# A hybrid transformer layer on one core: GpSimd's block sums, the banks of the down products, a chunk's final weighing and a weight split put elsewhere

## The chip, the cores and the metric

The kernel runs on one core of one Trainium2 chip. Its time is the device time of one execution in microseconds (us). A core has a matrix engine (TensorE, PE in the rows; PEld is its weight load), a vector engine (VectorE, DVE), a scalar engine (ScalarE, ACT), GpSimd (POOL) and SyncE (SP), which here issues all DMAs. Each engine takes its own instructions in order and waits on semaphores of the others. Matrix products land in PSUM, eight banks of 512 float32 columns on 128 partitions. GpSimd has no way to PSUM in this kernel.

## The reference

One encoder layer over 1024 prompt tokens and 64 sample tokens, all in float32. What follows the attention is what matters here:

```python
x = x + (1.0 + ada[2]) * (o @ w_o)
h = rmsnorm(x, g_ffn) * (1.0 + ada[4]) + ada[3]
f = (jax.nn.silu(h @ w_gate) * (h @ w_up)) @ w_down     # 1024 -> 2816 -> 1024
x = x + (1.0 + ada[5]) * f
y = rmsnorm(x, g_final)
```

## The kernel before

**Tokens and products.** x lies transposed, as eight tiles of 128 features (m or kt = 0 to 7), in three chunks c of 384, 384 and 320 tokens. Each float32 matrix product is made of three: every operand is split into a rounded high part and the rest (`whi`, `wlo` for a weight, `h`, `d` and so on for an activation), and PE adds high x high, low x high and high x low into one bank. A split of a weight is a cast on ScalarE (`whi`), then a subtraction on VectorE or GpSimd (`wlo`). A weight tile of 128 x 1024 or 128 x 512 elements comes by one or two DMAs into one of four `wraw` buffers, and the split parts rotate through three pairs of tiles.

**Output projection.** `out_block(g, mp, chunks, ...)` takes one 512 x 256 block of w_o, splits it (on GpSimd for the four blocks of the second half, `OPL`), and makes its products for the chunks named, 24 matmuls a chunk. At the end of it chunk 2's rows are normed for the FFN (`norm2_last`), while the blocks of chunk 1 and then those of chunk 0 are made, so that three blocks of w_o are loaded and split twice.

**First FFN pass, chunk 2.** Eleven groups g of two 128-wide FFN columns: gate and up products (24 matmuls each), `silu`, the product `d`, its split, then `down_begin` and eight `down_block`s, one for each m, of six matmuls. `down_begin` makes the first half of three blocks ahead, in the banks t, t, acc. VectorE adds the finished block into x (line 1202). In group 0 the rows of chunks 0 and 1 get their root-mean-square: `token_cols` sums over features on PE (bank u), VectorE and ScalarE make the reciprocal root, `spread` lays it over 128 partitions with PE. In the last group `weigh` squares and scales each finished x for the final norm, on ScalarE, with the sum of squares on GpSimd.

**Second FFN pass, chunks 0 and 1.** Eleven groups again. The two chunks and the two columns make 2 x 2 blocks, multiplied in seven products of 12 matmuls instead of eight (`Seven`, `Blocks`). The weights' side needs block sums, all on GpSimd: `sums_first` (lines 1320 and 1321), `sum2` (1324) and `sum4` (1327); `prep` then splits an operand (line 1166 on ScalarE, 1167 on VectorE). After the seven gate products come seven up products, i = 0 to 6, whose `evac` (lines 1362 to 1374) and `up` (1506: product with silu; 1508: cast; 1509: low part) make `d`. A low part is queued in `left` and issued at the next `later(left)`. Then 16 down blocks follow, chunk 1 first, bi = 0 to 15. The two splits of w_down stand in the up products: at i == 3 on VectorE, at i == 5 with its low part on GpSimd. `final_cols`, `final_last` and `final_tile` norm, transpose and write the output.

**Order.** Up to the FFN a scheduler of the framework sets each engine's order. From `in_order` on it is the order in which the code is written, for PE, ScalarE, VectorE and GpSimd, up to `in_order.__exit__`; what follows that is the scheduler's again. Banks are asked for by tag: z (three), t (two), acc, u, av (one each).

## Time and profile before

| | |
|---|---|
| time, median of 3 runs (lowest to highest) | 1706.82 us (1706.05 to 1712.06) |
| the profiled execution: its own time | 1706.56 us |
| its span on the core | 1704.8 us |
| busy: PE, PEld | 1561.3 us (92%), 1449.6 us (85%) |
| busy: DVE, ACT, POOL | 1129.8 us (66%), 808.6 us (47%), 850.6 us (50%) |
| TensorE clock granted, mean | 0.97 of full speed |
| matmuls | 9558 |

Times in the rows are microseconds from the start of the span. The attention ends at about 817 us, the output projection's second half and `norm2_last` run to about 876, the first FFN pass to about 1133, the second to about 1693, and the last output is written after that. Busy time of PE is modelled from pipelined matmuls, so a wait of PE is better read from the list of waits (who waited, for whom, how long in total, how many times, the longest) than from the busy share.

### The profile page before, as it was taken

To read this page: it belongs to the slowest core of one execution; us is meant where nothing else is said; L and a number is where in the kernel's file an instruction comes from. 1 tells how busy PE (TensorE), PEld (TensorE's weight loads), DVE (VectorE), ACT (ScalarE), POOL (GpSimd) and SP (SyncE) were. 2 spreads that over 40 slices of the span, in tenths; PEclk is the share of its full clock that TensorE was granted. 3 is DMA by queue.
4 is the path that set the end of the run, shared out by engine and by line. 5 is a ranking of instruction groups with operands and counts; after the bars stand their busy time and mean duration, and the time that the engine had idled before them with its cause. 6 is when DMAs were issued, how large, how long until landed. Compare 5 with 4: busy or idle time off the path is not lost. (4 is left out here: it accounts for less than half of the span.)

```text
span 1704.8 us, 26702 instructions
## 1 busy us (share of the span) xinstructions
PE 1561.3 (92%) x9558; PEld 1449.6 (85%) x9558; DVE 1129.8 (66%) x2042; ACT 808.6 (47%) x1687; POOL 850.6 (50%) x703
## 2 busy tenths in 40 slices
PE   8898998988999968998989999979999999999996
PEld 4697887867888857887979999978999999999996
DVE  5669777589457565677875666646666666666665
ACT  5466656576445544555454444443333332233335
POOL 2568778797667775764453444442332233223222
PEclk9999999999999978999999999989999999999998
DMA  9433333321443552453244545522222212122201
GB/s 306 162 99 106 101 95 91 89 79 47 126 119 100 156 149 61 125 169 104 80 136 122 148 148 149 149 65 81 75 74 62 64 48 75 50 75 75 74 26 75
DMA packets 224789, 176.26 MB, mean 103 GB/s; under 512 B 15536, under 2 KB 215120, under 8 KB 224656
## 3 DMA queue, kind: packets, MB, share of 16 engines
q1 hardware_dynamic: 224656, 174.54, 35.5%
q8 instruction: 76, 1.25, 0.3%
q14 instruction: 57, 0.47, 0.1%
HBM read 140.21 MB, written 27.08 MB: 98 GB/s over the span
## 5 line engine op out<-in xcount | busy, mean ns | idle before, releaser
L1166 ACT CAST whi<-wraw 128x512 fp32r<-128x512 f32 (+1 forms) x220 | 168.5, 790 | 198.6 <-PE acc_d L1181 163.1
L1167 DVE TENSOR_TENSOR wlo<-wraw,whi 128x512 fp32r<-128x512 f32 (+1 forms) x177 | 169.5, 974 | 93.6 <-ACT whi L1166 87.9
L1202 DVE SCALAR_TENSOR_TENSOR x<-acc_d,ada,x 128x256 f32<-128x256 f32 (+1 forms) x352 | 163.1, 496 | 81.4 <-PE acc_d L1181 80.1
L429 PE MATMUL acc<-h,whi 128*128 128x384 f32 (+1 forms) x576 | 199.8, 347 | 6.1 <-DVE kraw L502 3.2
L1179 PE MATMUL acc_d<-d,whi 128*128 128x384 f32 (+1 forms) x528 | 180.5, 342 | 25.2 <-ACT d L1508 12.5
L431 PE MATMUL acc<-h,whi 128*128 128x384 f32 (+1 forms) x576 | 193.5, 336 | 3.6 <-DVE h L406 3.5
L430 PE MATMUL acc<-h,wlo 128*128 128x384 f32 (+1 forms) x576 | 194.1, 337 | 0.0
L1352 PE MATMUL gu<-bT,whi 128*128 128x384 f32 x704 | 188.6, 339 | 2.9 <-ACT u L1366 2.9
L1167 POOL TENSOR_TENSOR wlo<-wraw,whi 128x1024 fp32r<-128x1024 f32 x43 | 106.4, 2475 | 164.7 <-ACT whi L1166 158.0
L1180 PE MATMUL acc_d<-d,wlo 128*128 128x384 f32 (+1 forms) x528 | 175.2, 332 | 2.2 <-POOL wlo L1167 2.2
L1181 PE MATMUL acc_d<-d,whi 128*128 128x384 f32 (+1 forms) x528 | 176.5, 334 | 0.0
L713 DVE TENSOR_TENSOR_SCAN kp<-kp 128x384 f32<-128x384 f32 (+4 forms) x104 | 139.6, 1349 | 39.1 <-ACT kp L709 37.0
L1320 POOL TENSOR_TENSOR s<-wraw 128x512 f32<-128x512 f32 x22 | 28.4, 1292 | 251.7 <-DMA wraw<-in_w_gate 126.5
L443 ACT CAST aT<-pt_a 128x384 fp32r<-128x384 f32 (+3 forms) x208 | 98.9, 481 | 80.8 <-PE pt_a L749 70.0
L755 DVE TENSOR_TENSOR aT<-pt_a,aT 128x384 fp32r<-128x384 f32 (+3 forms) x208 | 110.1, 536 | 38.0 <-ACT aT L443 37.1
L1179 PEld LDWEIGHTS acc_d<-d,whi 128*128 128x128 f32 x528 | 101.1, 191 | 38.1 <-ACT d L1508 16.0
L1352 PEld LDWEIGHTS gu<-bT,whi 128*128 128x128 f32 x704 | 129.6, 190 | 3.4 <-ACT u L1366 3.2
L749 PE MATMUL pt_a<-ident,a_t 128*128 128x128 f32 x608 | 104.1, 283 | 29.6 <-DVE aT L755 16.3
L717 POOL TENSOR_TENSOR a_t<-a_t,kp 128x383 f32<-128x383 f32 (+6 forms) x104 | 112.9, 1094 | 33.5 <-DVE kp L713 10.5
L429 PEld LDWEIGHTS acc<-h,whi 128*128 128x128 f32 x576 | 111.4, 193 | 11.0 <-DVE kraw L502 3.6
L1352 PE MATMUL gu<-bT,wlo 128*128 128x384 f32 x352 | 119.0, 338 | 0.0
L431 PEld LDWEIGHTS acc<-h,whi 128*128 128x128 f32 x576 | 111.5, 194 | 5.2 <-DVE h L406 4.8
(357 smaller groups left out, 4319.1 us busy)
## 6 DMA issues: line engine op xcount, KB each, us to landing
wraw<-in_w_gate SPq DMA_DIRECT2D x44, 512.0 KB, 4.0
wraw<-in_w_up SPq DMA_DIRECT2D x44, 512.0 KB, 3.9
wraw<-in_w_down SPq DMA_DIRECT2D x44, 512.0 KB, 3.6
lowraw<-in_w_ada SPq DMA_DIRECT2D x32, 512.0 KB, 3.8
wraw<-in_w_in SPq DMA_DIRECT2D x24, 512.0 KB, 6.2
wa<-in_w_ada SPq DMA_DIRECT2D x16, 512.0 KB, 6.3
oT_d<-ot SPq DMA_DIRECT2D x128, 64.0 KB, 2.6
wraw<-in_w_o SPq DMA_DIRECT2D x14, 512.0 KB, 3.8
```

The lines of the kernel that those rows point to most:

```text
L429: pe.matmul(out=acc, lhsT=wh[:, kt, :], rhs=rh[kt], start=st, stop=False)
L430: pe.matmul(out=acc, lhsT=wl[:, kt, :], rhs=rh[kt], start=False, stop=False)
L431: pe.matmul(out=acc, lhsT=wh[:, kt, :], rhs=rl[kt], start=False, stop=sp_)
L713: dve.tensor_tensor_scan(out=rev, data0=rev, data1=rev, initial=1.0 if b == w else kp[:, b:b + 1], op0=ALU.mult, op1=ALU.min)
L717: eng[E_AM[qt]].tensor_tensor(out=a_t[:, :wm], in0=a_t[:, :wm], in1=kp[:, a + 1:a + 1 + wm], op=ALU.mult)
L1166: act.copy(out=hi, in_=src)
L1167: lo_eng.tensor_tensor(out=lo, in0=src, in1=f32(hi), op=ALU.subtract)
L1179: pe.matmul(out=a_, lhsT=wh[:, m, :], rhs=dh, start=first, stop=False)
L1180: pe.matmul(out=a_, lhsT=wl[:, m, :], rhs=dh, start=False, stop=False)
L1181: pe.matmul(out=a_, lhsT=wh[:, m, :], rhs=dl, start=False, stop=not first)
L1202: dve.scalar_tensor_tensor(out=xc[:, a:b], in0=acc[:, a:b], scalar=ada[:, 5, m, s:s + 1], in1=xc[:, a:b], op0=ALU.mult, op1=ALU.add)
L1352: pe.matmul(out=acc, lhsT=w_[:, k, :], rhs=bh[BAND[i], k, r_], start=(i in (0, 1, 3) and k == 0 and j == 0), stop=(k == 3 and j == 2), ski ...
```

## The change

Seven edits:

- `DB` gives the down products four banks (t, t, acc, u), and `down_begin` begins four blocks.
- In the up products, the second split of w_down is cast at i == 4 and its low part is made by VectorE, not GpSimd (in the first pass's last group too: `lo_eng=dve if last`).
- `sums_first` of the next gate weights stands behind the first down block (bi == 0) instead of at up product i == 3; the two `prep`s stand at bi 3 and 5 instead of 1 and 2, and `sum2`, `sum4` at bi 6 instead of 3.
- Chunk 2's `weigh` leaves the last group of the first pass. Its 16 steps (`beside`) are issued one by one behind products of the second pass's first two groups, its additions on VectorE. `final_cols(2)` and `final_last` come in group 1 instead of 0.
- In group 0 of the first pass `rms_rows` is cut in two: the column sums behind m = 1 and 4 (bank av), the spreading behind m = 3 and 6.
- The blocks of w_o that chunks 1 and 0 share are loaded and split once.
- In the last group `in_order` ends after chunk 1's last block, and chunk 1's `final_cols` and output tiles are asked for there.

```diff
 HBW = 3
-NPG = (1, 3, 5, 7)
+DB = ("t", "t", "acc", "u")
 QT = (6, 7, 0, 1, 4, 5, 2, 3, 8)
...
-    def rms_rows(c, out=None):
+    def rms_cols(c, tag="u"):
+        col = opl.tile([P, 2, 9], F32, tag="col", name="col2")
+        token_cols([sacc[c]], chunk_toks(c), D, col, tag)
+        return col
+
+    def rms_rows(c, col, out=None):
...
         n = CH[c][1]
-        col = opl.tile([P, 2, 9], F32, tag="col", name="col2")
-        token_cols([sacc[c]], chunk_toks(c), D, col)
         bc = bank("t", "bc2")
...
         n = CH[2][1]
-        bc = rms_rows(2)
+        bc = rms_rows(2, rms_cols(2))
         for kt in range(KT):
...
         norm2_last()
-        for mp in range(3):
-            out_block(1, mp, (1,), fxh, fxl, evac_fox, tags)
     for mp in range(3):
-        out_block(1, mp, (0,), fxh, fxl, evac_fox, tags)
+        out_block(1, mp, (1, 0), fxh, fxl, evac_fox, tags)
     attB.close()
...
-            if sums[c] is None:
-                sums[c] = opl.tile([P, 384], F32, tag="sacc", bufs=3, name="sums")
-                act.activation(sums[c][:, :n], xc, AF.Square)
-            else:
-                sq = opl.tile([P, 384], F32, tag="sq", name="sq3")
-                act.activation(sq[:, :n], xc, AF.Square)
-                (dve if c == 0 and m % 2 else pool).tensor_tensor(
-                    out=sums[c][:, :n], in0=sums[c][:, :n], in1=sq[:, :n], op=ALU.add)
-            act.activation(xc, xc, AF.Copy, scale=gl[:, m:m + 1])
+            def square():
+                if sums[c] is None:
+                    sums[c] = opl.tile([P, 384], F32, tag="sacc", bufs=3, name="sums")
+                    act.activation(sums[c][:, :n], xc, AF.Square)
+                else:
+                    sq = opl.tile([P, 384], F32, tag="sq", name="sq3")
+                    act.activation(sq[:, :n], xc, AF.Square)
+                    (dve if c == 2 or (c == 0 and m % 2) else pool).tensor_tensor(
+                        out=sums[c][:, :n], in0=sums[c][:, :n], in1=sq[:, :n], op=ALU.add)
+
+            def scale():
+                act.activation(xc, xc, AF.Copy, scale=gl[:, m:m + 1])
+            return [square, scale]
...
-            for m in range(3):
-                begun[m] = bank(("t", "t", "acc")[m % 3], "acc_d")
+            for m in range(4):
+                begun[m] = bank(DB[m % 4], "acc_d")
                 down_products(begun[m], wd, dd, c, m, ahead, True)
...
             else:
-                acc = bank(("t", "t", "acc")[m % 3], "acc_d")
+                acc = bank(DB[m % 4], "acc_d")
                 down_products(acc, wd, dd, c, m, ahead, True)
...
             if last:
-                weigh(m, c, xc, n)
+                for f in weigh(m, c, xc, n):
+                    f()
...
             gu = gate_up("u", f1)
-            ready("d", f0, lo_eng=pool)
+            ready("d", f0, lo_eng=dve if last else pool)
             gated(f1, gu)
...
             for m in range(KT):
-                down_block(wd, dd, 2, m, last, 0)
+                down_block(wd, dd, 2, m, False, 0)
                 if m == 0 and not last:
...
                     first7.prep()
-                if g == 0 and m in (2, 5):
-                    rms_rows(m // 3, sacc[m // 3])
+                if g == 0 and m in (1, 4):
+                    col2 = rms_cols(m // 3, "av")
+                elif g == 0 and m in (3, 6):
+                    rms_rows(m // 3 - 1, col2, sacc[m // 3 - 1])
             if not last:
...
         cur7 = first7
+        beside = []
+        for m in range(KT):
+            beside += weigh(m, 2, x1[m][2], n2)
         for gi, g0 in enumerate(groups):
...
                     B.evac(i)
+                if beside and i > 1:
+                    beside.pop(0)()
             B = Blocks(up7, ("av", "z", "u"), up)
...
                 later(left)
-                if i == 0 and gi == 0:
+                if beside:
+                    beside.pop(0)()
+                if i == 1 and gi == 1:
+                    assert not beside
                     col2 = final_cols(2)
...
                     wd = [None, part(raws.pop(("d", 1)), *part_tiles())]
-                    if not last:
-                        nx7.sums_first()
-                elif i == 5:
-                    wd[0] = part(raws.pop(("d", 0)), *part_tiles(), pool)
+                if i == 4:
+                    raw = raws.pop(("d", 0))
+                    wd[0] = part_tiles()
+                    act.copy(out=wd[0][0], in_=raw)
                 B.evac(i)
+                if i == 4:
+                    dve.tensor_tensor(out=wd[0][1], in0=raw, in1=f32(wd[0][0]), op=ALU.subtract)
             down_begin(wd, dd, 1)
...
                 if not last:
-                    if bi in (1, 2):
+                    if bi == 0:
+                        nx7.sums_first()
+                    elif bi in (3, 5):
                         nx7.prep()
-                    elif bi == 3:
+                    elif bi == 6:
                         nx7.sum2()
                         nx7.sum4()
-                elif c == 0 and m == 2:
+                elif c == 1 and m == 7:
+                    in_order.__exit__(None, None, None)
                     col1 = final_cols(1)
-                elif c == 0 and m in (4, 5, 6):
-                    final_tile(col1, 1, m - 4)
-                if gi == 0 and c == 1:
+                    for j in range(3):
+                        final_tile(col1, 1, j)
+                if gi == 1 and c == 1:
                     if m in (3, 5, 7):
...
                 cur7 = nx7
-        in_order.__exit__(None, None, None)
         col0 = final_cols(0)
```

VectorE in a group of the second pass, from the sixth up product's first evictions to the first down blocks (m, u: products being assembled; sg: silu of the gate; d: the split product; x_0_1: m = 0 of chunk 1). Before:

```order
L1371 TENSOR_TENSOR m_14576<-m_14576,gu 128x384
L1506 TENSOR_TENSOR m_14439<-m_14439,m_14576 128x384
L1509 TENSOR_TENSOR d<-m_14439,d 128x384
L1374 TENSOR_TENSOR u_14554<-u_14554,gu 128x384
L1506 TENSOR_TENSOR u_14424<-u_14424,u_14554 128x384
L1509 TENSOR_TENSOR d<-u_14424,d 128x384
L1506 TENSOR_TENSOR sg<-sg,gu 128x384
L1509 TENSOR_TENSOR d<-sg,d 128x384
L1202 SCALAR_TENSOR_TENSOR x_0_1_9765<-acc_d,ada,x_0_1_9765 128x384
L1202 SCALAR_TENSOR_TENSOR x_1_1_9781<-acc_d,ada,x_1_1_9781 128x384
L1167 TENSOR_TENSOR wlo<-wraw,whi 128x512
L1202 SCALAR_TENSOR_TENSOR x_2_1_9863<-acc_d,ada,x_2_1_9863 128x384
```

and with the change:

```order
L1377 TENSOR_TENSOR m_14555<-m_14555,gu 128x384
L1517 TENSOR_TENSOR m_14421<-m_14421,m_14555 128x384
L1578 TENSOR_TENSOR wlo<-wraw,whi 128x1024
L1520 TENSOR_TENSOR d<-m_14421,d 128x384
L1380 TENSOR_TENSOR u_14536<-u_14536,gu 128x384
L1517 TENSOR_TENSOR u_14406<-u_14406,u_14536 128x384
L1520 TENSOR_TENSOR d<-u_14406,d 128x384
L1517 TENSOR_TENSOR sg<-sg,gu 128x384
L1520 TENSOR_TENSOR d<-sg,d 128x384
L1207 SCALAR_TENSOR_TENSOR x_0_1_9765<-acc_d,ada,x_0_1_9765 128x384
L1207 SCALAR_TENSOR_TENSOR x_1_1_9781<-acc_d,ada,x_1_1_9781 128x384
L1207 SCALAR_TENSOR_TENSOR x_2_1_9863<-acc_d,ada,x_2_1_9863 128x384
```

The low part of the second w_down split (`wlo<-wraw,whi 128x1024`, line 1578) now stands on VectorE between the assembly of the third block and its low part, ahead of the whole chain of `u`; the half-size `wlo` of the next gate weights have left the places behind x_1_1 and x_2_1.

GpSimd in the same stretch, with the semaphores that each row waits for. Before (`s`: the first block sum of the next gate weights; the two rows behind it complete one weight's sums but for the split between them):

```order
L1320 TENSOR_TENSOR s_14156<-wraw 128x512 [waits DMAHW0_49,DVE_49]
L1321 TENSOR_TENSOR wraw<-wraw 128x512 [waits DMAHW7_49,DVE_49,Pool_49]
L1167 TENSOR_TENSOR wlo<-wraw,whi 128x1024 [waits DMAHW6_49,Activation_49]
L1324 TENSOR_TENSOR wraw<-s_14156,wraw 128x512 [waits DVE_49,Pool_49]
L1327 TENSOR_TENSOR wraw<-wraw 128x512 [waits DVE_49,Pool_49]
```

and with the change:

```order
L1326 TENSOR_TENSOR s_14151<-wraw 128x512 [waits DMAHW1_49,DVE_49]
L1327 TENSOR_TENSOR wraw<-wraw 128x512 [waits DMAHW0_49,DVE_49,Pool_49]
L1330 TENSOR_TENSOR wraw<-s_14151,wraw 128x512 [waits DVE_49,Pool_49]
L1333 TENSOR_TENSOR wraw<-wraw 128x512 [waits DVE_49,Pool_49]
L1326 TENSOR_TENSOR s_14398<-wraw 128x512 [waits DMAHW3_49,DVE_49]
```

The split has gone, and the sums stand next to each other. The two rows of `sums_first` wait for their DMAs and for VectorE in both kernels, and for no engine that would tie them to the down products; what they wait for on VectorE are the last `wlo` that read the buffer `s` and the last `wlo` that read the `wraw` buffer.

VectorE at the end of the program, chunk 0's down blocks (x_0_0 to x_7_0) with the column chain of chunk 1 (L215 to L196) and its output tiles (`y`). Before:

```order
L1202 SCALAR_TENSOR_TENSOR x_2_0_9797<-acc_d,ada,x_2_0_9797 128x384
L215 TENSOR_SCALAR col_18094<-pc 128x3
L192 RECIPROCAL col_18094<-col_18094 128x3
L193 TENSOR_TENSOR col_18094<-col_18094 128x3
L194 TENSOR_TENSOR col_18094<-col_18094 128x3
L195 TENSOR_SCALAR col_18094<-col_18094 128x3
L196 TENSOR_TENSOR col_18094<-col_18094 128x3
L1202 SCALAR_TENSOR_TENSOR x_3_0_9813<-acc_d,ada,x_3_0_9813 128x384
L1136 TENSOR_TENSOR sums<-sums,sq_18114 128x384
L1202 SCALAR_TENSOR_TENSOR x_4_0_9901<-acc_d,ada,x_4_0_9901 128x384
L1297 TENSOR_SCALAR y<-py,col_18094 128x512
L1202 SCALAR_TENSOR_TENSOR x_5_0_9917<-acc_d,ada,x_5_0_9917 128x384
```

and with the change:

```order
L1207 SCALAR_TENSOR_TENSOR x_4_0_9901<-acc_d,ada,x_4_0_9901 128x384
L1138 TENSOR_TENSOR sums<-sums,sq_18115 128x384
L1207 SCALAR_TENSOR_TENSOR x_5_0_9917<-acc_d,ada,x_5_0_9917 128x384
L1207 SCALAR_TENSOR_TENSOR x_6_0_10005<-acc_d,ada,x_6_0_10005 128x384
L215 TENSOR_SCALAR col_18042<-pc 128x3
L192 RECIPROCAL col_18042<-col_18042 128x3
L193 TENSOR_TENSOR col_18042<-col_18042 128x3
L194 TENSOR_TENSOR col_18042<-col_18042 128x3
L195 TENSOR_SCALAR col_18042<-col_18042 128x3
L196 TENSOR_TENSOR col_18042<-col_18042 128x3
L1207 SCALAR_TENSOR_TENSOR x_3_0_9813<-acc_d,ada,x_3_0_9813 128x384
L1303 TENSOR_SCALAR y<-py,col_18042 128x512 x2
```

The chain stands behind seven of the eight blocks instead of three; block 3 has moved behind it, since its bank u holds the column sums until L215 has read them, and no `y` stands ahead of blocks 4 to 6 any more.

## Rows read from the trace of the kernel before

**Rows 1.** Windows: stretch, length; busy (count) of PE, PEld, DVE, ACT, POOL; clock, DMA.

```profile
842.00:898.00 56.00, 49.03 (x292) 45.99 (x291) 40.79 (x62) 27.80 (x50) 32.03 (x21) 1.00 0.42 124
...
1113.00:1160.00 47.00, 38.21 (x200) 36.89 (x199) 24.66 (x46) 23.04 (x44) 19.33 (x15) 0.89 0.24 68
...
1200.00:1660.00 460.00, 441.57 (x2471) 430.37 (x2470) 297.43 (x418) 152.85 (x284) 125.75 (x83) 1.00 0.22 63
1660.00:1705.00 45.00, 31.72 (x178) 29.21 (x176) 23.80 (x46) 25.12 (x45) 12.53 (x11) 0.86 0.18 71
```

**Rows 2.** Waits of PE, 842 to 898: output projection and first gate products.

```profile
PE acc_o L430 <- POOL wlo L178: 4.1, 3, 1.7
PE gu L430 <- DVE wlo L1167: 1.4, 2, 0.7
PE gu L429 <- ACT whi L1166: 0.9, 1, 0.9
```

**Rows 3.** Waits of PE, group 0 of the first FFN pass.

```profile
PE bc L223 <- DVE col L196: 3.5, 2, 1.9
```

**Rows 4.** Waits of PE, 1113 to 1160: from first pass to second.

```profile
PE acc_d L1179 <- DVE x L1202: 3.7, 2, 1.9
PE gu L1352 <- ACT u L1366: 2.9, 1, 2.9
PE acc_d L1180 <- POOL wlo L1167: 2.2, 1, 2.2
```

**Rows 5.** Waits of PE, nine groups of the second pass.

```profile
PE acc_d L1179 <- ACT d L1508: 11.5, 9, 1.5
PE acc_d L1179 <- DVE x L1202: 6.9, 16, 0.6
```

**Rows 6.** Waits of PE, the end.

```profile
PE py L1294 <- DVE y L1297: 3.3, 1, 3.3
```

**Rows 7.** Windows of PE alone: length, busy (matmuls), granted clock.

```profile
1129.00:1136.20 7.20, 6.18 (x22) 0.53 0.01 3
1142.60:1146.20 3.60, 3.60 (x13) 0.53 0.47 145
1272.40:1276.00 3.60, 3.60 (x13) 0.53 0.42 126
```

**Rows 8.** Timeline of one group; idle time before, and its releaser, in brackets.

```profile
1215.58 1.29 POOL L1320 TENSOR_TENSOR s<-wraw 128x512 f32<-128x512 f32 x1 [12.58 <-DMA wraw<-in_w_gate]
...
1215.82 0.55 DVE L1371 TENSOR_TENSOR m<-m,gu 128x384 f32<-128x384 f32 x1 [1.61 <-PE gu L1352]
...
1221.14 0.34 PE L1181 MATMUL acc_d<-d,whi 128*128 128x384 f32 x1
...
1222.27 0.44 PE L1179 MATMUL acc_d<-d,whi 128*128 128x384 f32 x1 [0.79 <-ACT d L1508]
```

**Rows 9.** Groups of GpSimd by form, 1200 to 1660.

```profile
L1320 POOL TENSOR_TENSOR s<-wraw 128x512 f32<-128x512 f32 x18 | 23.2, 1291 | 215.3 <-DMA wraw<-in_w_gate 108.1 <-DVE wlo L1167 107.3
L1167 POOL TENSOR_TENSOR wlo<-wraw,whi 128x1024 fp32r<-128x1024 f32 x9 | 21.5, 2384 | 14.8 <-ACT whi L1166 14.8
```

**Rows 10.** Timeline of VectorE, last group of the first pass.

```profile
1116.04 2.20 DVE L1167 TENSOR_TENSOR wlo<-wraw,whi 128x1024 fp32r<-128x1024 f32 x1
```

**Rows 11.** Groups of ScalarE by form, 1660 to the end.

```profile
L1138 ACT ACTIVATE x<-x,gl 128x384 f32<-128x384 f32 x16 | 9.9, 616 | 0.5
L1135 ACT ACTIVATE sq<-x 128x384 f32<-128x384 f32 x14 | 7.2, 514 | 5.3 <-DVE x L1202 4.7 <-DVE col L215 0.6
```

**Rows 12.** Groups of VectorE, 1200 to 1660: count, busy, mean ns, idle before.

```profile
L1506 DVE TENSOR_TENSOR u<-u,u 128x384 f32<-128x384 f32 x9 | 23.8, 2641 | 0.3
...
L1167 DVE TENSOR_TENSOR wlo<-wraw,whi 128x1024 fp32r<-128x1024 f32 x10 | 12.3, 1226 | 11.0 <-ACT whi L1166 11.0
...
L1509 DVE TENSOR_TENSOR d<-u,d 128x384 fp32r<-128x384 f32 x9 | 5.0, 559 | 5.2 <-ACT d L1508 5.2
```

**Rows 13.** DMA issues, 1200 to 1660: KB each, median us to landing.

```profile
wraw<-in_w_down SPq DMA_DIRECT2D x18, 512.0 KB, 3.6
```

## The prediction

> **What bounds the kernel now.** I read the windows by stage first [rows 1]. From 1200 to 1660 us PE is busy 441.57 of 460.00 us, VectorE 297.43, ScalarE 152.85: PE sets the time, and an edit can only win back PE's pauses. That stretch has 18.4 us of them, 1113 to 1160 has 8.8, the end (1660 to 1705) 13.3 and the output projection's second half 7.0. Next I read who ended PE's waits in each stretch. The reader should see few and always the same releasers: GpSimd's low parts of w_o [rows 2], the column chain [rows 3], then evictions, a late copy and one GpSimd split at the change of passes [rows 4], the cast of d and the evictions in the groups of the second pass [rows 5], a `y` at the end [rows 6]. Last I looked at stretches of half clock: after waits PE ran at 0.53 of full speed for some 3.5 us, twice near 1130 to 1146 and once at 1272 [rows 7].
>
> A wait costs a little more than its row says. In [rows 8] a matmul starts at 1221.14 and the next at 1222.27, 1.13 us instead of 0.18 (441.57 us / 2471 matmuls), so 0.95 is lost, while the row shows 0.79. I add 0.16 us to each wait.
>
> **The change, part by part.**
>
> *w_o split once.* Three loads, three casts and three GpSimd splits go. Three waits of 4.1 us in all stood for such splits [rows 2], 4.6 with restarts. A split of this size is 2.38 us of GpSimd [rows 9], with a cast ahead of it; PE had 24 matmuls x 0.168 us (49.03 / 292) = 4.0 us to cover both and now has 8.1, so these waits go whole. The first gate weights then arrive earlier, too: of the 2.3 us of waits on them (2.8 with three restarts) I take half, bounds none and all. Gain 6.0 us (4.6 to 7.4). The sums of squares for chunks 0 and 1 are the same additions as before.
>
> *Roots cut in two, group 0.* Two waits of 3.5 us, 3.8 with restarts [rows 3]. The chain itself stays; now PE has two blocks between its two ends, six matmuls (blocks begun ahead) the first time and twelve the second. At 0.168 us that hides 1.0 of 1.9 us and then all. Gain 2.7 (2.0 to 3.8).
>
> *Change of passes.* The 2.2 us wait for GpSimd's split goes, since VectorE makes that one; of it [rows 10] is the dear case, 2.20 us while GpSimd is at work, still done before PE has made the twelve products begun ahead. The two eviction waits (3.7 us) came from ScalarE and VectorE being held by `weigh` between the `prep`s, and the 2.9 us wait for the copy of u from the same work and from GpSimd's sums standing behind the sums of squares [rows 4]. With four restarts 9.4 us. The two slow stretches behind them hold 22 matmuls in 6.18 us and 13 in 3.60 [rows 7], 2.2 and 1.3 us over full speed. Together 12.9; I leave 0.9 for a rest of the copy's wait, since two `prep`s still need tiles that only the last down block frees. Gain 12 (8 to 12.9). The 16 `beside` steps are 9 us on ScalarE (8 x 0.514 and 8 x 0.616) and 4 on VectorE (7 x 0.559) [rows 11, 12], one step behind a product of 12 matmuls x 0.18 = 2.1 us, on engines with a third and more of the time free [rows 1]: nothing; without that cover they would cost those 4 us at most.
>
> *Groups of the second pass.* PE waits 11.5 us for d and 6.9 us for evictions in nine groups [rows 5]; with 25 restarts 22.4, or 2.5 a group, plus 1.3 for the slow stretch at 1272. Why d is late: `u<-u,u` takes 2641 ns, where an operation of the same size and also with both operands in SBUF takes 559 [rows 12]; GpSimd's 2.38 us split runs beside it. That split now goes to VectorE, 1226 ns alone [rows 12]. But the block sums do not move. GpSimd has nothing ahead of them and they wait for their DMA, as now (the 12.58 us of idle time at 1215.58 ended with it), so they start 0.24 us before the third block's assembly at 1215.82 as before [rows 8], and last two operations, 1291 ns each or a little more [rows 9]. So the product of that block still waits, and the new split behind it: I take 2.20 us for it [rows 10], bounds 1.23 and 2.5 (a whole sum and then its own time). From 1215.82: 0.6 assembly, 1.0 product (shut out till the first sum ends at 1216.87), 2.2 split, then low part, addition and product of u at 0.56 each, 1221.2; a cast of some 0.5, and u's high part is there at 1221.7, where PE now goes on at 1222.27. So the chain itself gains 0.6 us only. The rest comes from the fourth begun block, three matmuls or 0.53 us of PE: PE needs u at 1221.3 + 0.5 = 1221.8. The wait for the cast is gone, its low part may be 0.3 late, and of the eviction waits, which lose the two `prep`s between them and start 0.6 earlier, I leave 0.2. What remains is 0.5 us a group; 9 x 2.0 = 18, and 1.3 for the slow stretch. The first and the last group hold the same chain; I put 1.2 each (an estimate, half of a group's wait). Gain 21.7; bounds: 1.4 a group remaining (the split at 2.5, VectorE late by it) gives 12, nothing remaining 26.
>
> The Trainium skill, page "SBUF — State Buffer", section "Who interferes with whom", has the rule that speaks against this edit: a VectorE instruction with two SBUF inputs and a GpSimd instruction that reads SBUF shut each other out for a whole instruction, one with at most one SBUF input is free. The trace agrees where it can: 2641 against 559 ns above, and the assemblies out of PSUM stay at 0.55 beside the sums. By that rule the new split is shut out in every group, which is the first rival.
>
> *The end.* ScalarE's 16 scalings and 14 squares (0.616 and 0.514 us) set the pace, with 5.8 us of idle time between them [rows 11], most of it behind the column chain and the tiles between blocks, where PE waited 3.3 us [rows 6]. In the new order seven blocks precede the chain; block 3 waits for it, and block 7 for block 3's bank. I give ScalarE 4.2 of the 5.8 us (bounds 0: the chain now holds two blocks instead; and 5.8).
>
> *Moved at no cost:* the output of chunk 2 goes from group 0 to group 1, its transposes with it.
>
> Sum: 6.0 + 2.7 + 12 + 21.7 + 4.2 = 46.6 us off the profiled execution's 1706.56 us (span 1704.8, 1.8 around it; the median is 1706.82): **1660 us**.
>
> **Rivals.** *The lock stays the price of each group:* the sums and the new split shut VectorE out as the old one did, and 1.4 us a group remain. For it: the sums do not move. Against: in the other phase, DMA landing earlier, they are over before the split. Gain of that part 12, time 1670. *The end gives nothing or loses:* the column chain, now late, holds blocks 3 and 7, and every output tile comes close to the last. The part goes from +4.2 to -3, time 1667; together with the first rival 1677. *Slower:* the cast of the second w_down split now stands on ScalarE and its low part on VectorE ahead of u. If its DMA is late, all of u and the evictions queue behind it. It is asked for seven products, 7 x 2.1 = 15 us, before its use and lands in 3.6 us [rows 13], 11.4 us to spare. To lose 8.5 us in all it would have to hold each of eleven groups by (46.6 + 8.5) / 11 = 5.0 us, that is land 16.4 us later than now. *It does little:* waits that go are replaced by waits for bank u, which the fourth block shares with the up product; worth less than 9 us in all, 1698 or more. Against: u is read out three VectorE operations before the block needs it.
>
> **Chances and range.** Forecast (1648 to 1665) 0.63; the lock 0.2; the end, alone or with the lock, 0.1; little 0.05; slower 0.02. Lower bounds of the gains give 1706.6 - 26.6 = 1680 (4.6 + 2 + 8 + 12 + 0), upper ones 1651; a slow stretch at the end may go as well, so the range is 1648 to 1680. A difference of 0.5%, 8.5 us, is about what a measurement of this kernel tells from no change. Faster 0.95, same 0.03, slower 0.02.
>
> **What would show it.** In the profile after: no wait of PE for a low part of w_o; one column wait under 1.2 us in group 0; at the change of passes no eviction wait over 0.5 us and no half-clock stretch between them; `u<-u,u` near 560 ns; GpSimd's sums still starting on their DMA beside the sixth up product, not beside the down products; the new 128 x 1024 split on VectorE near 2 us, not 1.23; PE's waits in nine groups 3 to 7 us instead of 18.4; ScalarE's idle time at the end under 2.5 us. The forecast is wrong if the cast of d still ends a wait of PE in each group, or if VectorE's evictions end longer ones than now.

## The result, and the profile after

The changed kernel takes **1645.96 us** (median of 4 runs, 1643.72 to 1647.06) against 1706.43 for the kernel before: a ratio of 0.9638 (95% interval 0.9614 to 0.9663), 60.5 us less. I had said 46.6 us less, 1660, in a range of 1648 to 1680. The direction was right, the time is 2 us below the range, and 14 us of gain were not foreseen. The profiled execution has a span of 1643.5 us (own time 1645.32). Of the runs below, one execution of weigh_last was in a slow state of the chip (2940.76 us) and is left out.

Where the time came from is read by stages. Their bounds are the first gate product, down product or output projection product of each stage in the traces; "won" is the difference of the lengths, "forecast" my term. The first stage holds no edit, and in the fifteen traces read here it takes 724.8 to 730.2 us; so a difference of a few microseconds between two kernels is read from the stages that hold the edit, not from the total.

| stage | before | after | won | forecast |
|---|---|---|---|---|
| up to the first product of the output projection | 728.7 | 729.0 | -0.3 | 0 |
| from there to the first gate product | 146.3 | 141.1 | 5.2 | 6.0 with the next row |
| gate and up of group 0, first pass | 21.2 | 18.4 | 2.8 | |
| down products of group 0 (roots) | 15.0 | 10.7 | 4.3 | 2.7 |
| from there to the last group's down products | 206.7 | 204.7 | 2.0 | 0 |
| change of passes with groups 0 and 1 of the second | 121.3 | 105.4 | 15.9 | 15.2 (12 + 1.2 + 2.0) |
| groups 2 to 9 of the second pass | 395.1 | 369.8 | 25.3 | 17.3 (8 x 2.0 + 1.3) |
| last group and end | 70.4 | 64.4 | 6.0 | 5.4 (1.2 + 4.2) |

The windows of the changed kernel by stage (stretch, length, busy us and count of PE, PEld, DVE, ACT and POOL, granted clock, DMA share, GB/s), which answer to [rows 1]:

```profile
842.00:893.00 51.00, 49.66 (x309) 48.41 (x307) 36.27 (x70) 26.93 (x48) 26.88 (x18) 1.00 0.39 114
1085.00:1135.00 50.00, 49.44 (x308) 49.03 (x307) 33.56 (x67) 24.25 (x45) 18.54 (x12) 1.00 0.36 104
1200.00:1600.00 400.00, 399.32 (x2282) 397.91 (x2281) 260.89 (x395) 143.15 (x264) 96.82 (x68) 1.00 0.23 67
1600.00:1643.50 43.50, 34.99 (x206) 32.71 (x204) 24.80 (x49) 25.93 (x49) 10.13 (x10) 0.90 0.19 73
```

In the second pass PE now pauses 0.7 us in 400 where it paused 18.4 in 460, and the half-clock stretches of [rows 7] are gone: each of these windows ahead of the end has a granted clock of 1.00; the end has 0.90 (0.86 before). What is left of PE's waits from 842 to 1600 us (who waited, for whom, total, times, longest) answers to [rows 2 to 5]:

```profile
PE acc_d L1184 <- DVE h L1287: 2.1, 2, 1.4
PE gu L429 <- DVE x L1024: 1.1, 1, 1.1
PE gu L1358 <- ACT u L1372: 0.9, 2, 0.6
PE bc L223 <- DVE col L196: 0.8, 1, 0.8
PE acc_d L1186 <- DVE d L1520: 0.6, 1, 0.6
PE py L1280 <- DVE x L1207: 0.3, 1, 0.3
PE gu L430 <- DVE wlo L1172: 0.2, 1, 0.2
```

No wait for a low part of w_o is left, one column wait of 0.8 us instead of two of 3.5 in sum, no wait for the eviction of a down block and none for the cast of d; from 1210 to 1600 us PE has no wait at all, where I expected 3 to 7 us to remain in nine groups. The largest one (line 1287) belongs to chunk 2's output tiles, moved to group 1; in the kernel before, in group 0, the same operation (there line 1281) held PE for 0.9 us. New is the 1.1 us ahead of the first gate product (1.4 by the weight load's row, which names another releaser, a square on ScalarE). The weight load's rows, by which the account below goes, still show short waits in the down products:

```profile
PEld acc_d L1186 <- DVE d L1520: 1.5, 4, 0.9
PEld acc_d L1184 <- DVE x L1207: 1.3, 5, 0.5
```

GpSimd and VectorE in one of the groups (start, length, line, operation, tiles; idle before and its releaser), which answer to [rows 8]:

```profile
1372.56 1.29 POOL L1326 TENSOR_TENSOR s<-wraw 128x512 f32<-128x512 f32 x1 [11.87 <-DMA wraw<-in_w_gate]
1373.93 1.29 POOL L1327 TENSOR_TENSOR wraw<-wraw 128x512 f32<-128x512 f32 x1
```

```profile
1373.52 0.56 DVE L1377 TENSOR_TENSOR m<-m,gu 128x384 f32<-128x384 f32 x1 [1.61 <-PE gu L1358]
1374.11 1.53 DVE L1517 TENSOR_TENSOR m<-m,m 128x384 f32<-128x384 f32 x1
1375.56 1.21 DVE L1578 TENSOR_TENSOR wlo<-wraw,whi 128x1024 fp32r<-128x1024 f32 x1
1376.70 0.55 DVE L1520 TENSOR_TENSOR d<-m,d 128x384 fp32r<-128x384 f32 x1
1377.17 0.54 DVE L1380 TENSOR_TENSOR u<-u,gu 128x384 f32<-128x384 f32 x1
1377.74 0.56 DVE L1517 TENSOR_TENSOR u<-u,u 128x384 f32<-128x384 f32 x1
1378.88 0.56 DVE L1520 TENSOR_TENSOR d<-u,d 128x384 fp32r<-128x384 f32 x1 [0.58 <-ACT d L1519]
```

The sums still start on their DMA and lie beside the sixth up product; `u<-u,u` takes 0.56 us instead of 2.64 [rows 12].

### The profile page after: what moved, and what is told of

The parts are those of the page before. It is cut to its first block, busy times and chain, and to the rows that moved or that the text cites. A ratio compares the mean times of both kernels' runs of the same rounds, so it can differ in the third digit from the quotient of the medians.

```text
span 1643.5 us, 26653 instructions
## 1 busy us (share of the span) xinstructions
PE 1540.2 (94%) x9558; PEld 1441.8 (88%) x9558; DVE 1106.1 (67%) x2061; ACT 805.3 (49%) x1684; POOL 810.2 (49%) x681
## 4 chain that ended last, share of the span: by engine, by line
PE 61%; DVE 6%; POOL 2%; ACT 2%; DMA 2%; issue 2%; SPq 1%; POOLq 0%; ACTq 0%; DVEq 0%
PE gu L1358 19%; PE acc_d L1184 5%; PE acc_d L1186 5%; PE acc_d L1185 5%; PE gu L430 3%; PE gu L431 3%; PE gu L429 3%; PE acc L429 2%; PE acc L430 2%; PE acc L431 2%; PE ps_av L758 2%; PE pt_a L749 2%; PE acc_o L429 1%; PE acc_o L430 1%; PE acc_o L431 1%
## 5 line engine op out<-in xcount | busy, mean ns | idle before, releaser
L1171 ACT CAST whi<-wraw 128x512 fp32r<-128x512 f32 (+1 forms) x209 | 157.0, 776 | 183.9 <-PE acc_d L1186 146.4
L1172 DVE TENSOR_TENSOR wlo<-wraw,whi 128x512 fp32r<-128x512 f32 (+1 forms) x178 | 162.9, 931 | 84.9 <-ACT whi L1171 81.6
L1207 DVE SCALAR_TENSOR_TENSOR x<-acc_d,ada,x 128x256 f32<-128x256 f32 (+1 forms) x352 | 159.1, 494 | 66.5 <-PE acc_d L1186 65.7
L1184 PE MATMUL acc_d<-d,whi 128*128 128x384 f32 (+1 forms) x528 | 175.3, 332 | 3.0 <-DVE h L1287 2.1
L1186 PE MATMUL acc_d<-d,whi 128*128 128x384 f32 (+1 forms) x528 | 173.5, 329 | 0.6 <-DVE d L1520 0.6
L1172 POOL TENSOR_TENSOR wlo<-wraw,whi 128x1024 fp32r<-128x1024 f32 x31 | 76.8, 2477 | 125.3 <-ACT whi L1171 116.5
L758 PE MATMUL ps_av<-aT,vv 128*128 128x256 f32 x608 | 104.9, 295 | 9.2 <-DVE aT L755 5.6
```

Source lines behind the costliest of these rows:

```text
L758: pe.matmul(out=ps_av, lhsT=vv[:, v0 + j, :], rhs=aT[:, j, :], start=(ci == 0 and j == 0), stop=(ci == len(parts) - 1 and j == nb - 1))
L1171: act.copy(out=hi, in_=src)
L1172: lo_eng.tensor_tensor(out=lo, in0=src, in1=f32(hi), op=ALU.subtract)
L1184: pe.matmul(out=a_, lhsT=wh[:, m, :], rhs=dh, start=first, stop=False)
L1186: pe.matmul(out=a_, lhsT=wh[:, m, :], rhs=dl, start=False, stop=not first)
L1207: dve.scalar_tensor_tensor(out=xc[:, a:b], in0=acc[:, a:b], scalar=ada[:, 5, m, s:s + 1], in1=xc[:, a:b], op0=ALU.mult, op1=ALU.add)
```

## The experiments

The theory, after this trace: the sums' place does nothing; the split on VectorE (which shortens the chain of VectorE and ScalarE operations up to d) and the fourth bank (which gives PE more products to make meanwhile) together end all waits in the groups, and the size was wrong because I priced waits by PE's own rows (theory A in what follows). The rivals: the sums left VectorE's chain (B); the fourth bank alone (C).

**sums_i3**

```diff
                     wd = [None, part(raws.pop(("d", 1)), *part_tiles())]
+                    if not last:
+                        nx7.sums_first()
...
-                    if bi == 0:
-                        nx7.sums_first()
-                    elif bi in (3, 5):
+                    if bi in (3, 5):
```

> The changed kernel with GpSimd's first block sums asked for at up product i = 3 again, as in the kernel before; all else as changed. Theory A (the sums have no engine to wait for in either place, so the place in the code decides nothing; the second split of w_down on VectorE and the fourth bank made the gain): the same time, 1644 to 1648 us, the sums starting on their DMA in each group and u<-u,u at about 0.56 us. Theory B (the sums' new place took them off VectorE's chain): u<-u,u goes back above 1.2 us, the wait for the cast of d returns and costs 1 to 2 us in each of ten groups, so 1655 to 1668 us.

1646.36 us (ratio 0.9641, 0.9622 to 0.9661), groups 2 to 9 at 46.2 us in the mean as in the changed kernel. B falls: beside the other edits the sums' new place is worth nothing.

**pool_split**

```diff
-                if i == 4:
-                    raw = raws.pop(("d", 0))
-                    wd[0] = part_tiles()
-                    act.copy(out=wd[0][0], in_=raw)
+                elif i == 5:
+                    wd[0] = part(raws.pop(("d", 0)), *part_tiles(), pool)
                 B.evac(i)
-                if i == 4:
-                    dve.tensor_tensor(out=wd[0][1], in0=raw, in1=f32(wd[0][0]), op=ALU.subtract)
```

> The changed kernel with the low part of the second w_down split on GpSimd at i = 5 again, sums behind the first down block and four banks kept. Theory A: u<-u,u is shut out again (2.6 us), the chain to d ends 1.8 us later, PE waits 1.2 us for d in a group although four blocks are begun, and the evictions, 1.8 us later, end one or two waits more of about 0.8 us; with what PE loses behind each wait 2.2 to 2.9 us in each of eleven groups: 1670 to 1678 us. Theory B (what counts is that the sums left the chain): below 1655 us. Theory C (the fourth bank hides the whole chain however late): 1646 to 1652 us.

1657.01 us (0.9705, 0.9681 to 0.9730): 11 us lost, where A said 24 to 32, B at most 9 and C nothing or little. C falls, and A's size too. `u<-u,u` is shut out again, made to wait by GpSimd's instruction (2.75 us), but I had the rest of the chain from the kernel before, where the sums run ahead of the split. GpSimd in one group here:

```profile
1331.93 2.40 POOL L1172 TENSOR_TENSOR wlo<-wraw,whi 128x1024 fp32r<-128x1024 f32 x1 [15.55 <-ACT whi L1171]
1334.29 1.61 POOL L1326 TENSOR_TENSOR s<-wraw 128x512 f32<-128x512 f32 x1
```

The sums now queue behind the split, `m<-m,m` is not shut out (0.56 us), and the cast of d comes nearly in time (the weight load waits 0.3 us for it in each group). So with the split on GpSimd the sums' place does matter, which the next run tests.

**pool_split_i3** is pool_split with the edit of sums_i3 as well.

> The run pool_split (1657 us: the second w_down split's low part on GpSimd at i = 5, four banks), with the first block sums at i = 3 again, that is ahead of that split on GpSimd instead of behind it. Theory A (on GpSimd the order of the two decides when the split runs: behind the sums it is 2.7 us later and lies against u's chain, as in before_four, which loses 1.0 us a group more than pool_split): 1.0 us in each of ten or eleven groups, 1666 to 1669 us, m<-m,m shut out (about 1.6 us) as well as u<-u,u. Theory B (the sums' place never decides anything): 1655 to 1659 us.

1660.10 us (0.9715, 0.9699 to 0.9731), between B's range and A's. The stages tell more than the times: 47.9 us a group against 47.4, 0.5 of the 1.0 expected. Theory A has the sign and half the size, and B falls here; the sums' place is worth 0.5 us a group while the split is GpSimd's, nothing once it is VectorE's. The other 0.45 us to before_four (48.4) I put down to the `prep`s at bi 1 and 2, which stand ahead of evictions; `sum2` and `sum4` have another place in before_four, too, and no run tells these apart.

**three_banks**

```diff
-DB = ("t", "t", "acc", "u")
+DB = ("t", "t", "acc")
...
-            for m in range(4):
-                begun[m] = bank(DB[m % 4], "acc_d")
+            for m in range(3):
+                begun[m] = bank(DB[m % 3], "acc_d")
...
-                acc = bank(DB[m % 4], "acc_d")
+                acc = bank(DB[m % 3], "acc_d")
```

> The changed kernel with three banks for the down products and three blocks begun, as before. Theory A: the chain to d is as in the changed kernel, so the cast of d ends hardly a wait (0 to 0.3 us); but block 3 needs the bank of block 0, which VectorE frees only behind its chain, 1.1 us late, with what PE loses behind a wait 1.2 to 1.6 us in each of eleven groups of the second pass, and the 0.2 us a group of the first pass come back: 1661 to 1667 us. Theory C (the fourth bank alone made the gain of the groups): 3.2 us a group, 1678 us or more. Theory B: no wait in the groups, 1648 us or less.

1659.19 us (0.9722, 0.9703 to 0.9741), 2 us under A's numbers, far from B's and C's. 1.1 us a group come back as an eviction wait, and the 2.0 us of the first pass too (206.73 us up to the last group's down products). The waits of the weight load and of PE from 1240 to 1600 us, eight groups:

```profile
PEld acc_d L1184 <- DVE x L1207: 7.7, 8, 1.0
```

```profile
PE acc_d L1184 <- DVE x L1207: 5.1, 8, 0.6
```

**before_four** is the kernel before with the four banks (the reverse of the diff above) and the column sums of group 0 in bank av.

> The kernel before with four banks (t, t, acc, u) and four blocks begun, nothing else of the change (the column sums of group 0 take bank av, since block 3 holds u). Theory A: the 0.2 us of each first-pass group go (2 us); in the second pass PE needs d 0.53 us later, so the 1.3 us wait falls to about 0.75, and the eviction waits from 0.77 us a group to 0.3 to 0.6: 0.8 to 1.2 us in each of eleven groups, 11 to 15 us in all: 1691 to 1696 us. Theory C (the bank alone made the gain of the groups): 3.2 us a group, 1668 to 1672 us.

1693.94 us (0.9927, 0.9906 to 0.9949), in A's range: 1.0 us a group and the 2.0 us of the first pass (204.75).

**three_banks_late and late** hold the sums back in earnest, in the kernels with three and with four banks:

```diff
                     if bi == 0:
+                        held = fp.tile([P, 1], F32, tag="held", name="held")
+                        pool.tensor_copy(out=held, in_=x1[0][1][:, 0:1])
                         nx7.sums_first()
```

> The run with three banks (1659 us), and the block sums now truly held back: before them GpSimd copies one column of x of the first down block, so that they cannot start before VectorE has evicted it. Theory A (the sums beside the split cost VectorE about 1 us of its chain, and with three banks the evictions stand right behind that chain): the split takes 1.23 instead of 2.3 us, the eviction waits of about 1.2 us a group fall to 0.2 or none, 1647 to 1652 us. Rival (the sums beside the evictions slow these, so nothing is won): 1657 us or more.

> The changed kernel with the sums held back in the same way, four banks. Theory A (with four banks nothing waits for VectorE's chain any more): the split on VectorE takes 1.23 us, the time stays within 1642 to 1648 us. Rival (the shut-out split still costs something in each group): 2 to 8 us less, 1638 to 1643 us.

three_banks_late: 1654.31 us (0.9692, 0.9677 to 0.9706), between both. The split takes 1.22 us and the first eviction wait goes, but a low part at bi 3 is shut out by the late sums and an eviction behind it is late: 0.9 us a group instead of 1.1. late: 1643.32 us (0.9623, 0.9609 to 0.9637), in A's range and at the edge of the rival's. Groups 2 to 9 are the same (46.16 us each against 46.22), so the shutting out, 0.9 to 1.1 us in each group of the changed kernel, is hidden there but for 0.06 us. What is won, 2.8 us, lies in groups 0 and 1. The split and the product ahead of it in late, from 1200 to 1600 us:

```profile
L1578 DVE TENSOR_TENSOR wlo<-wraw,whi 128x1024 fp32r<-128x1024 f32 x8 | 9.7, 1219 | 0.0
L1517 DVE TENSOR_TENSOR m<-m,m 128x384 f32<-128x384 f32 x17 | 9.5, 559 | 0.6
```

**The price of a wait.** Eight kernels give it, for groups 2 to 9 (means of eight groups; waits from 1240 to 1600 us divided by the groups of down products in that stretch, 7 or 8):

| kernel | mean group | over late's 46.16 | waits of PEld | waits of PE |
|---|---|---|---|---|
| before | 49.39 | 3.23 | 3.23 | 2.07 |
| before_four | 48.36 | 2.20 | 2.46 | 1.09 |
| pool_split_i3 | 47.91 | 1.75 | 1.98 | 0.91 |
| pool_split | 47.38 | 1.22 | 1.44 | 0.40 |
| three_banks | 47.27 | 1.11 | 1.20 | 0.64 |
| three_banks_late | 47.04 | 0.88 | 0.99 | 0.46 |
| after | 46.22 | 0.06 | 0.10 | 0 |
| late | 46.16 | 0 | 0 | 0 |

The lost time goes with the waits of the weight load, within 0.3 us; PE's own rows fall short by 0.4 to 1.2 us wherever more than 0.1 us is lost.

**w_o_twice**

```diff
         norm2_last()
+        for mp in range(3):
+            out_block(1, mp, (1,), fxh, fxl, evac_fox, tags)
     for mp in range(3):
-        out_block(1, mp, (1, 0), fxh, fxl, evac_fox, tags)
+        out_block(1, mp, (0,), fxh, fxl, evac_fox, tags)
```

> The changed kernel with the three blocks of w_o that chunks 1 and 0 share loaded and split for each chunk, as before. Theory A (the output projection's 5.2 us and the 2.8 us up to the first down products are both this edit's): 8 us more, 1652 to 1656 us, with three waits of the weight load for GpSimd's low parts and the first gate weights late again. Rival (the first gate weights came earlier through another edit): 5 us more, 1650 to 1652 us.

1652.07 us (0.9676, 0.9659 to 0.9693). That is the border of the two ranges; the stages decide: 146.1 and 20.7 us, 7.2 of the 8.0 us given back. PE's waits for the low parts are those of [rows 2] again, those for the first gate weights are back with 1.2 of their 2.3 us:

```profile
PE acc_o L430 <- POOL wlo L178: 4.1, 3, 1.7
...
PE gu L430 <- DVE wlo L1174: 0.9, 2, 0.7
...
PE gu L429 <- ACT whi L1173: 0.3, 1, 0.3
```

**roots_whole**

```diff
-                if g == 0 and m in (1, 4):
+                if g == 0 and m in (2, 5):
                     col2 = rms_cols(m // 3, "av")
-                elif g == 0 and m in (3, 6):
-                    rms_rows(m // 3 - 1, col2, sacc[m // 3 - 1])
+                    rms_rows(m // 3, col2, sacc[m // 3])
```

> The changed kernel with column sums and spreading together behind m = 2 and 5, column sums in bank av. Theory A (the 4.3 us won in the down products of group 0 are this edit's, 1.4 us of it by the half-clock stretch that follows the two waits): two column waits of 1.5 to 2 us, a half-clock stretch of 3.4 us behind them, the stage back at 14.4 to 15.1 us, 1649 to 1651 us. By the forecast's term alone: 2.7 us more, 1648 to 1649 us, no half-clock stretch.

1647.63 us (0.9657, 0.9636 to 0.9677), too near for the times to tell; the stage goes from 10.7 back to 14.8 us, as A has it. The two column waits are back, and behind them the half clock (windows of PE: length, busy and matmuls, granted clock):

```profile
PE bc L223 <- DVE col L196: 3.5, 2, 1.9
```

```profile
898.10:901.50 3.40, 3.40 (x15) 0.50 0.00 0
```

**weigh_last and weigh_last_2** (one kernel; the stages and rows are those of weigh_last_2)

```diff
-                down_block(wd, dd, 2, m, False, 0)
+                down_block(wd, dd, 2, m, last, 0)
...
-        for m in range(KT):
-            beside += weigh(m, 2, x1[m][2], n2)
```

with the additions on GpSimd.

> The changed kernel with chunk 2's 16 weighing steps back in the last group of the first pass, behind each finished x, additions on GpSimd; the w_down split of that group stays on VectorE, and the output of chunk 2 stays in group 1. Theory A (the weighing held ScalarE and VectorE between the preps and made the eviction waits, the late copy of u and the half-clock stretches): the last down products of the first pass 4 to 7 us longer than 7.1, group 0 of the second pass 3 to 5 us longer, half-clock stretches near 1120 and 1135 again, 1653 to 1658 us. Rival (the wait for GpSimd's split alone made most of it): less than 3 us, 1646 to 1649 us.

> The same kernel as weigh_last, for its stages. Theory A: the last down products of the first pass 11 to 14 us instead of 7.1 with waits of the weight load for VectorE's evictions and a half-clock stretch near 1115 to 1125, group 0 of the second pass 46 to 49 us instead of 43.8; 1653 to 1658 us. Rival (all of it in group 0, by the late copy of u): last down products under 9 us, group 0 over 50 us.

1654.96 us (three executions) and 1654.62 (0.9693, 0.9679 to 0.9707), in A's range. The last down products take 11.0 instead of 7.1 us and group 0 49.7 instead of 43.8: 9.8 us, at A's lower bound in the first and 0.7 above its upper one in the second. Both rivals fall: the loss is not under 3 us, and it is not all in group 0. The waits of PE, and the clock behind them:

```profile
PE gu L1358 <- ACT u L1372: 4.3, 1, 4.3
PE acc_d L1184 <- DVE x L1207: 3.5, 2, 1.8
```

```profile
1112.00:1116.00 4.00, 4.00 (x16) 0.58 0.00 0
1122.00:1126.00 4.00, 4.00 (x15) 0.57 0.53 157
```

**end_before**

```diff
-                elif c == 1 and m == 7:
-                    in_order.__exit__(None, None, None)
+                elif c == 0 and m == 2:
                     col1 = final_cols(1)
-                    for j in range(3):
-                        final_tile(col1, 1, j)
+                elif c == 0 and m in (4, 5, 6):
+                    final_tile(col1, 1, m - 4)
...
                 cur7 = nx7
+        in_order.__exit__(None, None, None)
         col0 = final_cols(0)
```

> The changed kernel with the end in the order of before (column sums of chunk 1 behind chunk 0's block 2, its output tiles behind blocks 4, 5 and 6, the written order up to the last block), four banks. The forecast's term: 4.2 us longer, last group 68.6 us. Theory A (of the 6 us that the last group got shorter 3.2 are the same waits as in the other groups, the rest the new order): 2.5 to 3.2 us longer, last group 67 to 67.6 us instead of 64.4. Rival (the new order gives nothing): 64 to 65 us. In time 1647 to 1650 us, which this measurement hardly tells from the changed kernel; the stage in the trace decides.

1646.28 us (0.9648, 0.9623 to 0.9673), just under the range and not to be told from the changed kernel, as expected. The last group takes 67.7 us instead of 64.4, a hair above A's range, so the new order is worth 3.4 us, not 4.2; the column chain stands among PE's waits again:

```profile
PE acc_d L1184 <- DVE col L215: 1.2, 1, 1.2
PE pc L204 <- POOL sums L1138: 1.1, 1, 1.1
```

**best and best_2** go on from late:

```diff
-                py = bank("t", "py")
+                py = bank("z", "py")
```

and, in best alone, bank av instead of u for chunk 0's blocks 3 and 7 in the last group.

> The changed kernel with the sums held back (as in late), chunk 2's output tiles in banks z instead of t, and bank av instead of u for chunk 0's blocks 3 and 7 in the last group. Theory A (in group 1 blocks wait 2.1 us for the output tiles' banks; at the end blocks 3 and 7 wait for the column sums' bank): group 1 50 to 51.5 us instead of 52.7 to 54.5, the last group 63.4 to 64 instead of 64.4, with late's 2.8 us 4 to 6 us less than the changed kernel: 1639 to 1642 us. Rival (these waits are replaced by others of the same length): 1643 to 1647 us.

> The run best (1639 us) without its bank av for chunk 0's blocks 3 and 7: sums held back and chunk 2's output tiles in banks z. If the av bank lost the 1.0 us at the end (65.4 us against 64.4 in late), the last group is 64.2 to 64.6 us again and the time 1636 to 1640 us; if the loss was the scheduler's for another reason, the last group stays above 65 us.

best: 1638.85 us (0.9595, 0.9578 to 0.9611). Group 1 takes 50.1 us instead of 54.5 (52.7 in late), but the last group 65.4. Without bank av (best_2) it is 64.1 again, so that edit was a loss, and the time is 1638.56 us (0.9605, 0.9591 to 0.9619). By the stages best_2 wins 0.9 us in group 0, 4.4 in group 1 and 0.3 in the last group over the changed kernel; from 1135 to 1600 us one wait of the weight load is left:

```profile
PEld gu L1358 <- ACT u L1372: 0.7, 1, 0.7
```

The intervals of best_2 and of the changed kernel overlap by a little (up to 0.9619 the one, from 0.9614 the other), so the medians, 7.4 us apart, are not told apart with certainty; the stages are.

## Why the prediction was right and wrong

**The step that failed: "I add 0.16 us to each wait."** I took it from one pair of matmul starts in [rows 8], and it counts only the first matmul behind the wait. The same place in full, matmuls first, then weight loads:

```profile
1221.14 0.34 PE L1181 MATMUL acc_d<-d,whi 128*128 128x384 f32 x1
1222.27 0.44 PE L1179 MATMUL acc_d<-d,whi 128*128 128x384 f32 x1 [0.79 <-ACT d L1508]
1222.55 0.34 PE L1180 MATMUL acc_d<-d,wlo 128*128 128x384 f32 x1
1222.86 0.44 PE L1181 MATMUL acc_d<-d,whi 128*128 128x384 f32 x1
1223.14 0.33 PE L1179 MATMUL acc_d<-d,whi 128*128 128x384 f32 x1
1223.31 0.34 PE L1180 MATMUL acc_d<-d,wlo 128*128 128x384 f32 x1
```

```profile
1222.26 0.19 PEld L1179 LDWEIGHTS acc_d<-d,whi 128*128 128x128 f32 x1 [1.11 <-ACT d L1508]
...
1222.86 0.19 PEld L1181 LDWEIGHTS acc_d<-d,whi 128*128 128x128 f32 x1 [0.30 <-DVE d L1509]
```

The next three intervals are 0.28, 0.31 and 0.28 us instead of 0.175: 0.34 more. The weight load shows both: it waits 1.11 us where PE's row says 0.79, and 0.30 for d's low part, where PE has no row at all, since the matmul before is still drawn as running. In matmul starts the place costs 0.95 + 0.34 = 1.29 us; PE's row and my 0.16 make 0.95 of it. The advice ahead of the prediction, to read a wait of PE from the list of waits, holds for the weight load's list alone. All waits of the weight load in the nine groups of the kernel before, where I had read PE's in [rows 5]:

```profile
PEld acc_d L1179 <- ACT d L1508: 14.4, 9, 1.9
PEld acc_d L1179 <- DVE x L1202: 12.0, 16, 1.0
PEld acc_d L1181 <- DVE d L1509: 2.7, 9, 0.3
```

29.1 us, 3.23 a group, against my 22.4 and 2.5. It even stood in [rows 1]: PEld is busy 430.37 of 460.00 us, idle 29.6, where I read PE's 18.4. The Trainium skill points the same way, page "Perfetto Trace Analysis", section "Identifying the Most-Contended Engine": the busy share of matmuls is not a good measure of how close TensorE is to its limit, and the busy share of weight loads is to be used instead, beside the arithmetic done. The rows here agree: the weight load is idle for 29.6 us in nine groups, 3.3 a group, and 3.16 us were won in each of eight. The page speaks of shares of a stretch and not of single waits.

**Second pass, groups: 25.3 instead of 17.3 in groups 2 to 9.** Two terms were mis-sized. What the waits cost was 3.23 us a group and not 2.5: 5.8 us in eight groups. What remains is 0.06 to 0.1 us and not 0.5: 3.4 us. Against them stands the slow stretch at 1272, for which I counted 1.3 us; the group that holds it won 0.4 more than the mean, so 0.9 of them did not come (17.3 + 5.8 + 3.4 - 0.9 = 25.6). The mechanism was right: sums in place, `u<-u,u` no longer shut out, the fourth block as cover. One detail was not. I expected the product to be shut out (1.0 us) and the split behind it as well (2.2); in seven of the nine groups from 1 to 9 the product is (1.4 to 1.6), and the split takes 1.21, as above; in the other two it is the reverse, 0.56 and 2.32. So the chain from the third block's assembly to the end of u's product takes 4.8 or 4.9 us, 0.5 to 0.6 less than I had it. The rival in which the lock stays the price of each group falls: without the shutting out (late) a group is 0.06 us shorter. The rule of the Trainium skill that I cited, page "SBUF — State Buffer", section "Who interferes with whom", is borne out all the same: VectorE's product with both operands in SBUF takes 1.53 us beside the sums and 0.56 without them.

**First pass: 2.0 us not foreseen.** The fourth bank serves the first pass too, which I left out. No wait of PE stands there; the weight load has nine of 0.2 us from 924 to 1117 us in the kernel before:

```profile
PEld acc_d L1179 <- issue: 1.9, 9, 0.2
```

before_four and three_banks show it from both sides (204.75 and 206.73 us). I had put this stage at nothing without a reason.

**w_o: 8.0 instead of 6.0.** The three low parts cost 4.9 us by the weight load's waits, not 4.6, and the first gate weights, of which I had taken half, came in time but for 0.2 us; against that stands the new 1.1 us ahead of the first gate product. w_o_twice gives 7.2 of the 8.0 back; no run assigns the other 0.8.

**Roots: 4.3 instead of 2.7.** The waits were sized well: 0.8 us are left, as forecast (0.9). I had not counted the half-clock stretch behind them, 1.4 us of the 4.1 that roots_whole gives back (twelve matmuls 0.27 us apart there instead of 0.147). The stretch stood in the trace of the kernel before:

```profile
907.30:910.80 3.50, 3.50 (x15) 0.51 0.00 0
```

**Change of passes: 15.9 against 15.2** for the stages together; the parts are moved among them with the output of chunk 2. The sum came out, in part by luck. weigh_last_2 shows 9.8 us of it to be the weighing's, but the waits were priced too low here as well (by the weight load's rows 10.0 us instead of my 9.4 at the change of passes, and 3.2 instead of 2.5 in each group), and what the output tiles cost was left out: in group 1 they hold two of the down products' banks, and with banks z for them that group takes 50.1 us in best_2, 52.7 in late. Moving them was no loss by PE's rows: their waits (of the transposes and right behind them) were 3.1 us in group 0 of the kernel before and are 2.4 in group 1 now. No run puts the last group's split back on GpSimd, so that term, 2.2 us and a restart, is not tested.

**End: 3.4 us for the order instead of 4.2**, and 2.6 instead of 1.2 for the group before it. ScalarE's idle time ahead of scalings and squares fell from 5.8 [rows 11] to 0.2 us, but not all by the order: in end_before, which has the old order and the other edits, it is 4.0 us. The order takes away 3.8 of it and wins 3.4. The squares in end_before and in the changed kernel, 1600 us to the end:

```profile
L1137 ACT ACTIVATE sq<-x 128x384 f32<-128x384 f32 x14 | 7.2, 515 | 3.5 <-DVE x L1207 2.9 <-DVE col L215 0.6
```

```profile
L1137 ACT ACTIVATE sq<-x 128x384 f32<-128x384 f32 x14 | 7.1, 511 | 0.0
```

The range failed with the same step: its bound of 26 us for eleven groups, "nothing remaining", was itself made of PE's rows. By the median the range was missed by 2.0 us only, which is also what the first pass gave, a stage that I had put at nothing; either step alone would account for the miss.

## What to carry to other kernels

Price a wait of TensorE by the idle time of its weight load, not of its matmuls: here the first gave the lost time within 0.3 us a group in eight kernels, and the second missed a third of it or more wherever it was above 0.1 us. When an instruction is moved to another place in the code, ask what it waits for: these sums waited for a DMA and did not move, until something ahead of them in their own queue (a split) did. And where two edits ease one chain (a bank more, a shorter chain) neither gives the whole: 1.1 us a group were lost again without the bank, 1.2 without the split on VectorE, and 3.2 in the kernel before, which has neither, nor the later `prep`s and sums.

## What was not expected of the hardware

Half-clock stretches follow waits closely enough to be undone with them: 3.4 us at 0.50 of full speed behind two column waits of 3.5 us in sum, gone when they are cut to 0.8, back in roots_whole. One such stretch comes and goes near 1195 us, in the second pass's group 1: sums_i3, w_o_twice and pool_split_i3 have it (that group takes 55.8 to 56.1 us), the changed kernel has not (54.5), though w_o_twice has the same code there. And the engine that is shut out need not be VectorE: in two groups of the changed kernel the second of the sums took 2.15 and 1.70 us instead of 1.29, while VectorE's product ran at its own 0.56.
